# Hybrid decoder layer: transposes of the values and of some probabilities by GpSimd pieces and VectorE in place of TensorE

## The chip, the cores and the metric

One core of one Trainium2 chip runs the whole layer. The metric is the device time of one execution in microseconds, the median of several runs. One of the executions is recorded by the hardware profiler, and all durations of single instructions come from that one.

## The reference

One decoder layer on x of 2048 tokens by 1024 columns, all in float32. Cut to what matters:

```
h = rmsnorm(x, norm_pre_g);  z = h @ w_in                      # 1024 -> 4096 columns
q, k, v, g_attn, c_h, c_b, c_c, g_conv = split(z)              # 4 x 768 and 4 x 256 columns
q, k = rope(q), rope(k)                                        # 12 heads of 64
for window, dilation in ((128, 1), (512, 4), (2048, 16)):
    o_i, lse_i = dilated_window_attn(q, k, v, window, dilation)  # causal, keys at distance 0, d, .., window
o = sum(softmax(lse)_i * o_i)
attn_out = o * silu(g_attn)
conv_out = c_b * causal_conv3(c_c * c_h, conv_w) * silu(g_conv)
out = x + rmsnorm(concat(attn_out, conv_out) @ w_out, norm_post_g)
```

## The kernel before, in words

The tokens are cut into four chunks of 512 (b = 0 to 3 in the code, chunks 1 to 4 in the text), the columns of w_in into eight groups of 512. A unit is one group on one chunk, 32 in all, numbered n = 4 * group + chunk. Groups 0 and 7 are convolution units. Groups 1 to 6 are attention units: each has k, q, v and the gate of one pair of heads, so 24 units, p = 0 to 5 pairs on four chunks.

**Number format.** Operands of the large products are split into two parts, high and low, by a copy on ScalarE that rounds and a subtraction on VectorE that keeps the rest. A product is then three matmuls: high by high, high by low, low by high (L1072, L1073, L1074 for the input projection, L1241 to L1243 for the output projection, which uses seven products in place of eight on 2x2 blocks).

**An attention unit** (`attn_unit`, L669). The projection leaves k, q, v and gate in four PSUM banks. k and q are rotated on VectorE and GpSimd (L707, L711), split (L717, L718, L722, L723), and q is copied in another order of tokens by GpSimd (L727). v is copied to `vz` (L696, L698), transposed by four TensorE transposes of 128x128 into a PSUM bank (L739), and split from there by ScalarE and VectorE (L744, L745) into `v2`, which also goes to DRAM and comes back in another order as `v1` (L749, L752). Scores are made on TensorE with 64 rows per head (L772, L800), masked with a running minimum on VectorE (L779, L807) and exponentiated on ScalarE (L783, L811).

The three patterns are handled as two kinds of probabilities. Kind 1 is pattern 1, the window of 128: tiles `p1`, four blocks of 128 queries by 256 keys. Kind 4 are patterns 2 and 3 jointly, where keys that belong to both count twice: tiles `p4`, four residues by up to 512 keys. Both have queries on partitions, and the product with the values wants keys there, so they are transposed:

- `parts` (L818) does kind 4. Blocks of the two nearest chunks go through four TensorE transposes into a PSUM bank (L840) and are split from PSUM (L845, L846). Blocks further back (`far`, chunks 3 and 4 only) go without TensorE: their entries lie so that a transpose within 32x32 blocks by VectorE, in place in SBUF (L831), is enough, and they are split from SBUF (L832, L833).
- `square` (L851) does kind 1. The previous block is subtracted from the current one (L853), which is possible because the masks leave complementary triangles; one transpose per pair of blocks then serves both (L863), and ScalarE's Relu with scale 1 and -1 (L870) with a maximum and a minimum on VectorE (L873, L877) takes them apart from PSUM again.

The products with the values are L889 to L902, their results are gathered by L920, L923 and L925, weighted (L1017, L1018), joined and gated on GpSimd (L1019, L1020) and stored.

**What sets the order.** A planner (`Plan`, L131) takes every operation with an engine, an estimated duration, a priority and the tiles that it reads and writes, and simulates the five queues (TensorE, ScalarE, VectorE, GpSimd and SyncE's DMAs). The order that comes out is written out as a fixed order per engine. A table SHIFT (L119) moves priorities by place in the code and by unit; operations marked `port` are kept apart from each other in the plan. Projections of the next units fill TensorE between the steps of an attention unit. Eight PSUM banks (`st`) serve everything; the values' and probabilities' parts sit in rings of five (`v2`), three (`v1`) and three (`pt`), the convolution's work tile `u` exists once.

**The start.** The first weight tile is one DMA on SyncE's queue (L462), cast as a whole by ScalarE (L469) and subtracted by VectorE (L470); the first matmuls (L1061) need it and the first tile of x (L490). The remaining parts of x follow on SyncE's queue (L518).

Of the kernel before, what the change touches and what calls it, by code (L numbers as in the profile page):

```python
# [37 lines left out]
VISIT = 2  # L38
KT = D // 128
# [73 lines left out]
class Op:  # L113
# [230 lines left out]
def dmat(kb):  # L344
    return max(0.5, kb / 352.0)
# [3 lines left out]
def hybrid_layer(ctx: ExitStack, tc: tile.TileContext, x, w_in, w_out, conv_w, g_pre, g_post,  # L349
                 rope, consts, out):  # L350
    nc = tc.nc
# [96 lines left out]
    W, w_last = {}, []  # L448

    def weights_in(grp, i):  # L450
# [5 lines left out]
        if grp in (0, 7):  # L456
            W[grp, i] = w
            if grp or i:
                add("DMA", dmat(256), pr, lambda: nc.sync.dma_start(raw.ap, w_in[i, :, grp, :]), w=[raw], land=6.0 if grp else 3.6)
            else:  # L460

                add("DMA", dmat(256), -1.995e6, lambda: nc.sync.dma_start(raw.ap, w_in[i, :, grp, :]), w=[raw], land=3.6)  # L462
# [204 lines left out]
    first_attn = []  # L667

    def attn_unit(n, p, b, zs):  # L669
# [64 lines left out]
        ps, v2, v1 = Tok(st_r), Tok(v2_r), Tok(v1_r)  # L734
        V2[u], V1[u] = v2, v1

        def vt():
            for r in range(4):
                nc.tensor.transpose(ps.ap[:, r * 128:(r + 1) * 128], vz.ap[:, r * 128:(r + 1) * 128], ident)  # L739
        add("PE", 0.44, pr, vt, r=[vz, "cst"], w=[ps, (v2, "hold")], mode=2)  # L740

        def src():
            return ps.ap.rearrange("p (r h d) -> p r h d", r=4, h=2)
        add("ACT", actt(C, True), pr + URG, lambda: act.copy(v2.ap[:, :, 0:4:3, :], src()), r=[ps], w=[(v2, 0)])  # L744
        add("DVE", dvet(C), pr + URG, lambda: vec.tensor_tensor(  # L745
            v2.ap[:, :, 1:3, :], src(), f(v2.ap[:, :, 0:4:3, :]), op=ALU.subtract), r=[ps, (v2, 0)], w=[(v2, 1)])
# [70 lines left out]

        def parts(h, kind, blk, far=False):  # L818
            pt, m, pp = Tok(pt_r), len(blk), P[h, kind]
            tiles = sorted({a for a, _ in blk})  # L820
            if far:
# [7 lines left out]
                def cut(a):  # L829
                    return a.rearrange("p a (c q) -> p a c q", q=128)  # L830
                add("DVE", dvet(m * 128) + 0.05, pr, lambda: vec.transpose(src(), src()), w=[(pp, a) for a in tiles])  # L831
                add("ACT", actt(m * 128), pr + URG, lambda: act.copy(dst(0), cut(src())), r=[(pp, a) for a in tiles], w=[(pt, 0)])  # L832
                add("DVE", dvet(m * 128), pr + URG, lambda: vec.tensor_tensor(dst(1), cut(src()), f(dst(0)), op=ALU.subtract),  # L833
                    r=[(pp, a) for a in tiles] + [(pt, 0)], w=[(pt, 1)], port=True)
# [16 lines left out]
        def square(h):  # L851
            pp, ps, first = P[h, 1], Tok(st_r), int(b == 0)
# [8 lines left out]
            def tr():  # L861
                for g in range(4):
                    nc.tensor.transpose(ps.ap[:, g * 128:(g + 1) * 128], pp.ap[:, g, 128:], ident)  # L863
            add("PE", 0.436, pr, tr, r=[(pp, g) for g in range(4)] + ["cst"], w=[ps] + [(pt, "hold") for pt in two], mode=2)

            def p4(lo):
                return ps.ap[:, lo * 128:].rearrange("p (i c) -> p i c", c=128)
# [487 lines left out]
```

## Time and profile before

| What | us |
|---|---|
| median of 3 runs (lowest, highest) | 1165.99 (1165.15, 1166.27) |
| the profiled execution | 1165.18 |
| its span, first to last instruction | 1163.1 |
| TensorE busy | 1152.5 |
| VectorE busy | 960.3 |
| ScalarE busy | 668.2 |
| GpSimd busy | 199.7 |

The profile calls TensorE's matmuls PE and its weight loads PEld, VectorE DVE, ScalarE ACT, GpSimd POOL and SyncE SP. Busy time is the union of the recorded intervals of an engine. Matmuls are pipelined, so that their intervals overlap and a busy PE is not at its peak; what an instruction costs in a stream is better read from the distance of starts. A row of the groups gives line, engine, operation, tiles and shapes, count, then busy time and mean duration in ns, then idle time of the engine just before and what ended it. A row of the timeline gives start and duration.

The stretch from about 130 to 950 us holds the attention units, the time before it the first convolution group and the loading of x, the time after it the output projection. The granted TensorE clock of the profiled execution is 0.998.

### The profile page before, as it was taken

The page shows a single profiled execution, that of the slowest core. Times are in us where ns is not written, and L with a number is a line of the kernel's source. Part 1 is how long each engine was busy: PE and PEld are TensorE (multiplying, and loading weights), DVE is VectorE, ACT ScalarE, POOL GpSimd, SP SyncE. Part 2 cuts the span into 40 slices and gives each one's busy share as a digit, 9 for nine tenths or more (in the row PEclk, how much of TensorE's full clock was granted, in tenths as well). Part 3 has the DMA queues.
Part 4 walks back from the last instruction along what each step waited for, and adds up shares of the span by engine and source line. Part 5 has one row for each costly group of instructions (what it writes and reads, how often), then busy time and mean ns, then how long its engine had stood idle before and what let it go on. Part 6 is the DMA issues. An engine that isn't in the chain of part 4 may idle for free.

```text
span 1163.1 us, 19964 instructions
## 1 busy us (share of the span) xinstructions
PE 1152.5 (99%) x6422; PEld 958.3 (82%) x6422; DVE 960.3 (83%) x2424; ACT 668.2 (57%) x1722; POOL 199.7 (17%) x158
## 2 busy tenths in 40 slices
PE   9999999999999999999999999999999999999997
PEld 7888888888888888888888888888888888888885
DVE  4744588997999989898999998997999888688876
ACT  6743365665666556666665565674667454544442
POOL 0001112212131222121223221203222103000000
PEclk9999999999999999999999999999999999999999
DMA  9977786787688767777777767688776968445452
GB/s 345 391 278 261 247 247 212 226 236 230 203 247 269 234 215 227 238 223 242 232 245 229 252 167 247 204 272 260 228 243 199 318 208 297 156 149 178 152 165 91
DMA packets 174136, 269.39 MB, mean 232 GB/s; under 512 B 53584, under 2 KB 109904, under 8 KB 174032
## 3 DMA queue, kind: packets, MB, share of 16 engines
q1 hardware_dynamic: 173472, 267.85, 71.1%
q8 instruction: 51, 0.84, 0.3%
q14 instruction: 53, 0.43, 0.1%
q10 hardware_dynamic: 560, 0.27, 0.1%
HBM read 206.77 MB, written 48.69 MB: 220 GB/s over the span
## 4 chain that ended last, share of the span: by engine, by line
PE 94%; DVE 2%; ACT 2%; DMA 1%; SPq 0%; issue 0%; POOL 0%; DVEq 0%; POOLq 0%; ACTq 0%
PE st L1072 20%; PE st L1074 19%; PE st L1073 19%; PE st L889 5%; PE st L1241 4%; PE st L1243 4%; PE st L1242 4%; PE st L772 4%; PE st L800 3%; PE st L840 3%; PE st L901 2%; PE st L863 2%; PE st L548 1%; PE st L902 1%; PE st L739 1%; PE st L900 1%
## 5 line engine op out<-in xcount | busy, mean ns | idle before, releaser
L1072 PE MATMUL st<-xt,w 128*128 128x512 f32 x1020 | 413.3, 405 | 0.0
L1074 PE MATMUL st<-xt,w 128*128 128x512 f32 x1020 | 399.7, 392 | 0.0
L1073 PE MATMUL st<-xt,w 128*128 128x512 f32 x1020 | 398.3, 391 | 0.0
L1074 PEld LDWEIGHTS st<-xt,w 128*128 128x128 f32 x1020 | 191.5, 188 | 42.4
L1072 PEld LDWEIGHTS st<-xt,w 128*128 128x128 f32 x1020 | 191.9, 188 | 40.4 <-issue 6.7
L1073 PEld LDWEIGHTS st<-xt,w 128*128 128x128 f32 x1020 | 192.1, 188 | 31.1
L783 ACT ACTIVATE p<-p,sm 128x128 f32<-128x128 f32 (+3 forms) x192 | 105.9, 553 | 69.2 <-DVE sm L779 69.0
L925 DVE TENSOR_TENSOR uu<-st,uu 64x256 f32<-64x256 f32 x288 | 115.0, 418 | 26.0 <-ACT uu L920 21.8
L920 ACT COPY uu<-st 64x256 f32<-64x256 f32 x192 | 67.2, 367 | 100.7 <-PE st L889 55.9
L1019 POOL TENSOR_TENSOR uu<-uu 128x512 f32<-128x512 f32 x24 | 37.4, 1557 | 359.0 <-DVE uu L1018 359.0
L811 ACT ACTIVATE p<-p,e 128x256 f32<-128x256 f32 (+1 forms) x192 | 94.4, 495 | 5.0 <-DVE e L807 4.8
L779 DVE CUSTOM_DVE_ANT_0 p<-st,cst 128x128 f32<-128x128 f32 (+3 forms) x192 | 82.1, 485 | 16.1 <-PE st L772 15.7
L889 PEld LDWEIGHTS st<-pt,v 128*128 128x128 f32 x480 | 66.7, 191 | 5.6
L807 DVE CUSTOM_DVE_ANT_0 p<-st,cst 128x256 f32<-128x256 f32 (+1 forms) x192 | 66.8, 412 | 4.2 <-PE st L800 4.2
L889 PE MATMUL st<-pt,v 128*128 128x256 f32 x480 | 68.5, 283 | 0.0
L870 ACT ACTIVATE pt<-st 128x512 fp32r<-128x512 f32 (+1 forms) x96 | 51.1, 585 | 24.2 <-PE st L863 20.7
L707 DVE TENSOR_TENSOR rp<-rp,cs 128x512 f32<-128x512 f32 x72 | 53.7, 772 | 12.9 <-DMA rp<-rp 12.7
L707 POOL TENSOR_TENSOR rp<-rp,cs 128x512 f32<-128x512 f32 x24 | 39.5, 1646 | 143.1 <-DMA rp<-rp 96.9
L846 DVE TENSOR_TENSOR pt<-st,pt 128x512 fp32r<-128x512 f32 x84 | 55.9, 683 | 5.0 <-ACT pt L845 4.7
L772 PE MATMUL st<-kk,q 64*128 64x128 f32 (+3 forms) x576 | 56.3, 333 | 0.3 <-DVE v L745 0.2
L772 PEld LDWEIGHTS st<-kk,q 64*128 64x128 f32 x576 | 42.4, 185 | 15.1 <-issue 10.8
L845 ACT CAST pt<-st 128x512 fp32r<-128x512 f32 x84 | 46.8, 581 | 9.0 <-PE st L840 8.4
(262 smaller groups left out, 2045.6 us busy)
## 6 DMA issues: line engine op xcount, KB each, us to landing
xt<-xt SPq DMA_DIRECT2D x256, 512.0 KB
raw<-in_w_in SPq DMA_DIRECT2D x59, 256.0 KB
rp<-rp SPq DMA_DIRECT2D x192, 64.0 KB
vd<-v SPq DMA_DIRECT2D x24, 512.0 KB
v<-vd SPq DMA_DIRECT2D x96, 128.0 KB
ab<-ad SPq DMA_DIRECT2D x48, 256.0 KB
cs<-in_rope SPq DMA_DIRECT2D x19, 512.0 KB
uu<-mix SPq DMA_DIRECT2D x26, 256.0 KB
```

Source lines behind the costliest of these rows:

```text
L707: add(e, dur, pr, lambda o=o, a=a, i=i, eng=eng: eng.tensor_tensor(o.ap, a.ap, cs.ap[:, i], op=ALU.mult), r=[cs], w=[o], port=True)
L772: mm(ps[h].ap[:, (r - r0) * w:(r - r0 + 1) * w], Q.ap[lo:lo + 64, i, r * 128:(r + 1) * 128], KK[j][lo:lo + 64, 4 * r:4 * r + 4, 0:w // 4]. ...
L779: add("DVE", dvet(w) + 0.01, pr + URG, lambda h=h, r=r, P4=P4: vec.tensor_tensor_reduce(P4.ap[:, r, 0:w], ps[h].ap[:, (r - r0) * w:(r - r0 ...
L783: add("ACT", actt(w) + 0.19, pr, lambda h=h, r=r, P4=P4: act.activation(P4.ap[:, r, 0:w], P4.ap[:, r, 0:w], AF.Exp, bias=s4(0, h)[:, r:r + ...
L807: add("DVE", dvet(256) + 0.01, pr + URG, lambda h=h, j=j, g=g, P1=P1: vec.tensor_tensor_reduce(P1.ap[:, g, lo[g]:], ps[h].ap[:, j * 256 + ...
L811: add("ACT", actt(256 - lo[g]) + 0.19, pr, lambda h=h, g=g, P1=P1: act.activation(P1.ap[:, g, lo[g]:], P1.ap[:, g, lo[g]:], AF.Exp, bias=E ...
L889: mm(dst, v, pt.ap[:, i], start=c == 0, stop=c == b, skip_group_check=False)
L920: add("ACT", actt(256, True) + 0.09, pr + URG, lambda: act.copy(cols(a, lo), o()[hi:hi + 64, 0]), r=[O], w=[(a, (h, half))])
L925: fn = lambda l=l: vec.tensor_tensor(cols(a, lo), o()[lo:lo + 64, l], cols(a, lo), op=ALU.add)
L1072: mm(z.ap, w.ap[:, 0, js], xt.ap[:, 0], start=kt == 0, stop=False)
L1073: mm(z.ap, w.ap[:, 0, js], xt.ap[:, 1], start=False, stop=False)
L1074: mm(z.ap, w.ap[:, 1, js], xt.ap[:, 0], start=False, stop=kt == KT - 1)
```

## The change

Sixty groups of four TensorE transposes are replaced: the values of all 24 units, kind 1 of chunks 2 and 3 (24 squares), kind 4 of chunk 1 (12 tiles). In each, a tile of 128 partitions by four blocks of 128 columns is transposed in two steps. GpSimd copies sixteen pieces, each 32 partitions by four runs of 32 elements, so that the 32x32 blocks stand in each other's places; then VectorE transposes within the 32x32 blocks, in place. The parts are split from SBUF instead of PSUM. For the values the intermediate tile is the convolution's `u`; for the probabilities it is a part of the same `p1` or `p4` tile that is free by then. Kind 1 of chunks 1 and 4 and the near blocks of kind 4 in chunks 2 to 4 stay on TensorE.

Besides, the first weight tile is loaded in two halves, by SyncE's and ScalarE's queues, and its rounded parts are made by ScalarE and VectorE, half each; the load of g_pre moves behind the first x load on ScalarE's queue; a projection may be planned only behind all scores of the unit two before it; and the table SHIFT is a new one (65 entries, 58 before).

```diff
+MOVE = 0.37
+SWAP = "POOL"
+ONE, FOUR = (1,2,), (0,)
...
+                for h, (en, queue) in enumerate((("DMA", nc.sync), ("ACT", nc.scalar))):
+                    cl = slice(256 * h, 256 * h + 256)
+                    add(en, 0.45, -1.995e6, lambda cl=cl, queue=queue: queue.dma_start(raw.ap[:, cl], w_in[0, :, 0, cl]), w=[(raw, h)], land=3.2,
+                        data=0.0 if h else 0.4)
+                    eng, fn = (("ACT", act.copy), ("DVE", vec.tensor_copy))[h]
...
-        ps, v2, v1 = Tok(st_r), Tok(v2_r), Tok(v1_r)
+        v2, v1 = Tok(v2_r), Tok(v1_r)
...
-        def vt():
-            for r in range(4):
-                nc.tensor.transpose(ps.ap[:, r * 128:(r + 1) * 128], vz.ap[:, r * 128:(r + 1) * 128], ident)
-        add("PE", 0.44, pr, vt, r=[vz, "cst"], w=[ps, (v2, "hold")], mode=2)
+        vq = Tok(u_r)
+
+        def flat():
+            return vq.ap[:, 0:4].rearrange("p r c -> p (r c)")
+
+        def cells(t):
+            return t.rearrange("p (r c a) -> p r c a", r=4, c=4)
+        for c in range(4):
+            for a in range(4):
+                add("POOL", MOVE, pr, lambda a=a, c=c: pool.tensor_copy(
+                    cells(flat())[32 * a:32 * a + 32, :, c, :], cells(vz.ap)[32 * c:32 * c + 32, :, a, :]), r=[vz], w=[(vq, (a, c))])
+        add("DVE", dvet(C) + 0.05, pr, lambda: vec.transpose(flat(), flat()), w=[vq])
...
+        def swap(pp, src, dst):
+
+            def quarters(o):
+                return pp.ap[:, :, o:o + 128].rearrange("p g (c a) -> p g c a", c=4)
+            for c in range(4):
+                for a in range(4):
+                    add(SWAP, MOVE, pr, lambda a=a, c=c: (act.copy if SWAP == "ACT" else pool.tensor_copy)(
+                        quarters(dst)[32 * c:32 * c + 32, :, a], quarters(src)[32 * a:32 * a + 32, :, c]), r=[(pp, g) for g in range(4)], w=[(pp, ("q", a, c))])
+            add("DVE", dvet(C) + 0.05, pr, lambda: vec.transpose(pp.ap[:, :, dst:dst + 128], pp.ap[:, :, dst:dst + 128]),
+                w=[(pp, ("q", a, c)) for a in range(4) for c in range(4)] + [(pp, "t")])
...
+            elif b in FOUR:
...
+                for k in range(4):
+                    for a in range(4):
+                        add(SWAP, MOVE, pr, lambda a=a, k=k: (act.copy if SWAP == "ACT" else pool.tensor_copy)(
+                            split(place())[32 * k:32 * k + 32, :, :, a], split(given())[32 * a:32 * a + 32, :, :, k]),
+                            r=[(pp, x) for x in tiles], w=[(pp, ("q", half, a, k))], after=away)
+                add("DVE", dvet(C) + 0.05, pr, lambda: vec.transpose(place(), place()),
...
+            if b in ONE:
+                swap(pp, 128, 0)
+                ps = (pp, "t")
...
-    add("ACT", 0.45, -2.1e6, lambda: nc.scalar.dma_start(gp, g_pre), w=["gp"], land=4.0)
+    add("ACT", 0.45, -1.996e6, lambda: nc.scalar.dma_start(gp, g_pre), w=["gp"], land=3.6)
...
-              done = add("PE", 3 * mmt(C), n * 100 + 50 + (kt if conv else j // 2 * 4 + kt / 2), proj, r=[xt, w], w=[zs[j]])
+              done = add("PE", 3 * mmt(C), n * 100 + 50 + (kt if conv else j // 2 * 4 + kt / 2), proj, r=[xt, w], w=[zs[j]], after=scored.get(n - 2, ()))
```

More of the change, by code (lines that the diff above doesn't have):

```diff
@@ L445, in hybrid_layer @@
     URG = -1.0e5
-    W, w_last = {}, []
+    W, w_last, XW = {}, [], []
     def weights_in(grp, i):
@@ L460, in weights_in @@
             else:
-                add("DMA", dmat(256), -1.995e6, lambda: nc.sync.dma_start(raw.ap, w_in[i, :, grp, :]), w=[raw], land=3.6)
+                for h, (en, queue) in enumerate((("DMA", nc.sync), ("ACT", nc.scalar))):
[3 more added lines that the diff above has]
+                    eng, fn = (("ACT", act.copy), ("DVE", vec.tensor_copy))[h]
+                    XW.append(add(eng, actt(256) if h == 0 else dvet(256), URG - 151.9, lambda cl=cl, fn=fn: fn(w.ap[:, 0, cl], raw.ap[:, cl]), r=[(raw, h)], w=[(w, h)]))
+                w_last[:] = [add("DVE", dvet(C) + 0.01, pc, lambda: vec.tensor_tensor(w.ap[:, 1], raw.ap, f(w.ap[:, 0]), op=ALU.subtract),
+                                 r=[raw, (w, 0), (w, 1)], w=[(w, 2)], after=XH, port=True)]
+                return
         else:
@@ L731, in attn_unit @@
         products = ((0, 0), (0, 1), (1, 0))
-        ps, v2, v1 = Tok(st_r), Tok(v2_r), Tok(v1_r)
+        v2, v1 = Tok(v2_r), Tok(v1_r)
         V2[u], V1[u] = v2, v1
-        def vt():
-            for r in range(4):
-                nc.tensor.transpose(ps.ap[:, r * 128:(r + 1) * 128], vz.ap[:, r * 128:(r + 1) * 128], ident)
-        add("PE", 0.44, pr, vt, r=[vz, "cst"], w=[ps, (v2, "hold")], mode=2)
+        vq = Tok(u_r)
[8 more added lines that the diff above has]
+        add("DVE", dvet(C) + 0.05, pr, lambda: vec.transpose(flat(), flat()), w=[vq])
         def src():
[L743 to L746, printed above, removed]
+            return vq.ap[:, 0:4].rearrange("p r (h d) -> p r h d", h=2)
+        add("ACT", actt(C), pr, lambda: act.copy(v2.ap[:, :, 0:4:3, :], src()), r=[vq], w=[(v2, 0)])
+        add("DVE", dvet(C), pr, lambda: vec.tensor_tensor(
+            v2.ap[:, :, 1:3, :], src(), f(v2.ap[:, :, 0:4:3, :]), op=ALU.subtract), r=[vq, (v2, 0)], w=[(v2, 1)], port=True)
         d, dk = v_d[u % 2], ("vd", u % 2)
@@ L851, in square @@
         def square(h):
-            pp, ps, first = P[h, 1], Tok(st_r), int(b == 0)
+            pp, first = P[h, 1], int(b == 0)
             add("DVE", dvet(C), pr, lambda: vec.tensor_tensor(
@@ L859, in blocks, with p4, tr @@
                 return pts[:, sorted((pt_r.index(t.slot) for t in two), reverse=True)[s]]
[L861 to L867, printed above, removed]
+            if b in ONE:
+                swap(pp, 128, 0)
+                ps = (pp, "t")
+                def p4(lo):
+                    return pp.ap[:, lo:, 0:128]
+            else:
+                ps = Tok(st_r)
+                def tr():
+                    for g in range(4):
+                        nc.tensor.transpose(ps.ap[:, g * 128:(g + 1) * 128], pp.ap[:, g, 128:], ident)
+                add("PE", 0.436, pr, tr, r=[(pp, g) for g in range(4)] + ["cst"], w=[ps] + [(pt, "hold") for pt in two], mode=2)
+                def p4(lo):
+                    return ps.ap[:, lo * 128:].rearrange("p (i c) -> p i c", c=128)
+            on = b in ONE
             for s, pt in enumerate(two):
                 lo = first if not s else 0
-                add("ACT", actt((4 - lo) * 128, True), pr + URG, lambda lo=lo, s=s: act.activation(
-                    blocks(s)[:, lo:, 0, :], p4(lo), AF.Relu, scale=1.0 if s else -1.0), r=[ps], w=[(pt, 0)])
+                add("ACT", actt((4 - lo) * 128, not on), pr + URG, lambda lo=lo, s=s: act.activation(
+                    blocks(s)[:, lo:, 0, :], p4(lo), AF.Relu, scale=1.0 if s else -1.0), r=[ps], w=[(pt, 0)] + [(pt, "hold") for pt in two if on])
                 if s:
```

37 lines of the change are left out of this document (30 added, 7 removed), and 17 rows, old and new, of the table SHIFT.

## The prediction

> **What bounds the kernel now.** I read the page first: the busy shares and the chain that ended last.
>
> ```profile
> span 1163.1 us, 19964 instructions
> PE 1152.5 (99%) x6422; PEld 958.3 (82%) x6422; DVE 960.3 (83%) x2424; ACT 668.2 (57%) x1722; POOL 199.7 (17%) x158
> ...
> PE 94%; DVE 2%; ACT 2%; DMA 1%; SPq 0%; issue 0%; POOL 0%; DVEq 0%; POOLq 0%; ACTq 0%
> ```
>
> TensorE (PE) is busy 99% of the span and carries 94% of the chain. A busy PE need not be a PE at its peak, and a share of the whole span hides stages, so next came the windows: the stretch in which the attention units run (130 to 950 us), two short stretches inside it, and three successive units of one head pair. Columns: length, then PE, PEld, DVE, ACT and POOL busy us, then clock, DMA share, GB/s.
>
> ```profile
> 130.00:950.00 820.00, 819.35 (x4909) 684.34 (x4908) 727.01 (x1927) 504.34 (x1411) 178.58 (x143) 1.00 0.75 236
> 338.00:398.00 60.00, 60.00 (x353) 50.11 (x350) 58.09 (x138) 39.74 (x103) 13.64 (x10) 1.00 0.78 241
> 340.00:370.00 30.00, 30.00 (x168) 25.17 (x167) 29.48 (x66) 19.35 (x49) 7.25 (x6) 1.00 0.77 242
> 668.60:766.80 98.20, 98.20 (x600) 82.43 (x599) 86.34 (x235) 60.69 (x176) 21.67 (x18) 1.00 0.71 217
> ```
>
> In those 820 us PE lacks 0.65 us of being always busy: projection matmuls fill every hole, so work taken off PE there shortens the run, as long as nothing else becomes late. VectorE (DVE) is the next: 727.0 of 820 (88.7%), and for a while 58.09 of 60 (96.8%) or 29.48 of 30 (98.3%), with PE still full. GpSimd (POOL) has room: 178.6 of 820.
>
> **The change part by part: PE.** 24 units lose the four transposes of the values (L739). Of the squares (L863), chunks 2 and 3 of six head pairs with two heads, 24, lose four each. Of the joint probabilities (L840), chunk 1 with six pairs and two heads, 12, lose four each. That is 60 groups, 240 transposes. What a group costs is read from starts, since the recorded durations overlap. The timeline of PE, once without and once with a group between two L1074:
>
> ```profile
> 342.49 0.39 PE L1074 MATMUL st<-xt,w 128*128 128x512 f32 x1
> ...
> 343.17 0.39 PE L1074 MATMUL st<-xt,w 128*128 128x512 f32 x1
> ```
>
> ```profile
> 328.58 0.40 PE L1074 MATMUL st<-xt,w 128*128 128x512 f32 x1
> 328.81 0.60 PE L739 MATMUL st<-cst,rp 128*128 128x128 f32 x4
> ...
> 329.71 0.40 PE L1074 MATMUL st<-xt,w 128*128 128x512 f32 x1
> ```
>
> Three matmuls on from one L1074 is the next: 0.68 us without, 1.13 us with four transposes between. A group costs 0.45 us, 0.11 a transpose, and 60 groups 27.0 us. The busy time of these lines gives a little more (0.149 a transpose), because it counts tails under which the next matmul already runs:
>
> ```profile
> L863 PE MATMUL st<-cst,p 128*128 128x128 f32 x192 | 28.7, 272 | 0.0
> ```
>
> The Trainium skill, "TensorE: Matmul & The Clock Gate", Part 4, gives about 275 ns for one transpose inside a kernel; the 272 ns in this row agree. By that figure the estimate would be 66 us for 240. The starts decide here: 272 ns is the time through the array, and only 0.11 us of it holds up the next instruction.
>
> **VectorE.** Each group brings one transpose of 128x512 within 32x32 blocks, as chunks 3 and 4 have it at L831. The subtractions that follow read SBUF in place of PSUM:
>
> ```profile
> L831 DVE STREAM_TRANSPOSE p<-p 128x512 f32<-128x512 f32 x36 | 24.3, 696 | 0.6 <-ACT p L783 0.5
> ...
> L846 DVE TENSOR_TENSOR pt<-st,pt 128x512 fp32r<-128x512 f32 x84 | 55.9, 683 | 5.0 <-ACT pt L845 4.7
> ...
> L833 DVE TENSOR_TENSOR pt<-p,pt 128x512 fp32r<-128x512 f32 x36 | 26.4, 735 | 0.2
> ...
> L845 ACT CAST pt<-st 128x512 fp32r<-128x512 f32 x84 | 46.8, 581 | 9.0 <-PE st L840 8.4
> ...
> L832 ACT CAST pt<-p 128x512 fp32r<-128x512 f32 x36 | 22.1, 614 | 2.6 <-PE st L889 2.3 <-DVE p L831 0.2
> ```
>
> 24.3/36 = 0.675 us of busy time each, times 60: 40.5 us. L833 (from SBUF) means 735 against 683 at L846 (from PSUM); the 52 ns are not the source but a wait for POOL, next paragraph. ScalarE's copies get 33 ns dearer (614 against 581); 84 of them make 2.8 us on an engine that is busy 504 of 820 us, so nothing on the path, and at most 2.8 if that cover went.
>
> **The port between VectorE and GpSimd.** A DVE operation with two SBUF inputs and a POOL instruction exclude each other, single-input copies included:
>
> ```profile
> 361.16 0.61 POOL L727 CAST q<-q 128x512 fp32r<-128x512 f32 x1 [1.21 <-ACT q L722]
> ...
> 361.31 1.01 DVE L723 TENSOR_TENSOR q<-rp,q 128x512 fp32r<-128x512 f32 x1
> ```
>
> ```profile
> 421.40 1.67 POOL L1019 TENSOR_TENSOR uu<-uu 128x512 f32<-128x512 f32 x1 [21.01 <-DVE uu L1018]
> ...
> 421.84 1.78 DVE L707 TENSOR_TENSOR rp<-rp,cs 128x512 f32<-128x512 f32 x1
> ...
> 423.03 1.74 POOL L707 TENSOR_TENSOR rp<-rp,cs 128x512 f32<-128x512 f32 x1
> ```
>
> The copy ends at 361.77 and the DVE operation 0.55 us later; its undisturbed time is that of L846, 0.68, so the first 0.13 of a wait is hidden. In the second pair DVE ends at 423.62, again 0.55 after POOL's end, and the next POOL instruction waits: DVE gets the port at every hand-over, so a DVE operation waits for the rest of one copy, not for a row of sixteen.
>
> The change adds 960 copies (60 groups of 16, each 32 partitions by 128 elements). The trace has no such copy. From below stands a POOL instruction that writes one element per partition (102 ns), from above the copy of 512 elements over all partitions (median 617):
>
> ```profile
> L1346 POOL MEMSET const-bfloat16-1.0<- 128x1 bf16 x1 | 0.1, 102 | 0.0
> ```
>
> ```profile
> L727 POOL CAST q<-q x48: 611/617/1532, 133.0 to 898.4; 128x512 fp32r<-128x512 f32 x48
> ```
>
> A straight line between them gives 0.23 us at 128 elements. The planner books 0.37 (MOVE) and books 0.647 for L727, where the row has 0.617, so its POOL costs are good to 5%; I take 0.37 and keep 0.23 and 0.617 as ends. From the code, about 410 DVE operations with two SBUF inputs would run in the stage: eight per unit (192), 48 each at L470 and L853, 36 at L833, some 16 smaller groups' and the 84 subtractions that lose PSUM. With copies of length c the port is taken 960c of 792 us, and the mean excess of an operation that meets one is (c - 0.13) squared over 2c. At 0.37: 0.45 x 0.078 x 410 = 14 us. At 0.23: 2 us; at 0.617: 59 us.
>
> So DVE comes to 727.0 + 40.5 + 14 = 781.5 us, while PE needs 819.4 - 27.0 = 792.4: DVE would have to be busy 98.6% of the shorter stage. The trace shows it busy 96.8% for 60 us and 98.3% for 30 us with PE full, never that for the whole stage. I take the middle, 97.5%: 781.5/0.975 = 801.5 us, 18.5 less than now. PE then waits about 9 us that it did not wait before, for scores' banks and transposed probabilities that DVE delivers late.
>
> **GpSimd's own time and what queues behind it.** The row of three units above is chunks 1 to 3 of one pair. They get 48 copies each, 144 x 0.37 = 53 us on 21.7, so 75 of about 94 us. A copy that meets one of DVE's two-input operations (410 x 0.55 of 792 us, 28%) waits some 0.27 us, which makes it 0.445 on average: 86 of 94 us. Full, but not over. Behind the copies in POOL's order stand the rotation of q (L707, L711, L727) and the final combination (L1019, L1020); PE's scores wait for the first, nothing near waits for the second. The values now reach SBUF after 16 copies, a transpose and the split, some 6 us later than after 0.45 us of PE; SyncE waits for them at L749 already, and behind it stand the loads of the x tiles:
>
> ```profile
> SPq L749 <- DVE v L745: 25.4, 11, 5.5
> ```
>
> If the planner's order allows for 0.37 a copy, that is no cost; each copy 0.075 late makes 1.2 us per unit.
>
> **The rest.** Splitting the first weight load over two queues and engines lets the copy L469 end some 0.3 us earlier and so L490, for which the first matmul waits. But the chain then goes through the x load:
>
> ```profile
> 5.32 0.62 ACT L469 CAST w<-raw 128x512 fp32r<-128x512 f32 x1 [2.15 <-DMA raw<-in_w_in]
> ...
> 5.85 0.47 ACT L490 ACTIVATE xt<-st,gp 128x256 fp32r<-128x256 f32 x1
> ```
>
> ```profile
> 6.13 4.68 DMA p<-in_x
> ```
>
> PE stands until that lands (10.81), so I put 0, between -0.5 and +0.5 (the later g_pre). The 60 PSUM banks set free gain nothing while PE lacks 0.65 us. The edge from scores to the projection two units on lies within PE and holds no semaphore: 0. The new table of shifts reorders everything; it can gain at most those 0.65 us, and what it loses is in the range.
>
> Sum: span 1163.1 - 18.5 = 1144.6. The profiled execution took 1165.18, 2.1 around its span, and the median is 0.8 above it: 1166.0 - 18.5 = 1147.5 us.
>
> **The rivals.** (a) PE alone decides, DVE keeps up at 98.6%: 1166.0 - 27.0 = 1139. For it: the 30 us at 98.3%. Against it: no longer stretch holds that. (b) DVE takes all back: if it can hold no more than 781.5/820 = 95.3% over the stage, the time stays at 1166. Against it: the 60 us at 96.8%. (c) GpSimd becomes the bound, and slower: in chunks 1 to 3 it needs 144c + 21.7 us where the stage now has 98.2. From c = 0.53, waits included, it loses. At 0.55 it is 100.9, 2.7 over, times six pairs 16: 1182 us. For it: 0.445 is estimated and the 512-element copy takes 0.617; against it: a quarter of the elements. (d) The port is held for the whole of a copy and none of the wait is hidden: 0.45 x 0.185 x 410 = 34 us, DVE 801.5; at 97.5% the stage is 822, at 96.8% 828, so 1168 to 1174. Against it: L723 above ended 0.55, not 0.68, after the copy. The Trainium skill, "SBUF — State Buffer", "SBUF: two separate sides", has it so: an exclusive lock for the whole instruction, the loser fully blocked; the exclusion agrees with the rows, the full block does not quite. (e) SyncE's queue stands 1.2 us per unit longer at L749 and the x tiles come late by as much: 24 x 1.2 = 29, so 1147.5 + 29 = 1176.5. Against it: x tiles are fetched well ahead. That the transposes stay on PE can't be: the code drops them.
>
> **How the numbers follow.** DVE decides, 1141 to 1156 (781.5/0.983 = 795 and 781.5/0.968 = 807 us give 1141 and 1153, and the contention's upper end a little more): 0.47. (a) 0.24, (b) 0.08, (c) 0.11, (d) 0.05, (e) 0.05. Time 1147.5, range 1137 to 1178: outside lie (c) and the low edge of (a), about 0.15. About 0.2% is what a measurement here can tell from no change. Faster by more: 0.47 + 0.24 = 0.71; within: 0.08; slower: 0.11 + 0.05 + 0.05 = 0.21.
>
> **What would show it.** Right: L739 gone, L863 at 96 and L840 at 288; PE's lack in the attention stage grown from 0.65 us to about 9, ended by DVE (or by ACT behind it); DVE at 97 to 98% there; POOL's copies about 0.37 us with gaps, POOL busy near 600 us. Wrong: PE still without holes (a); POOL without gaps in chunks 1 to 3 and PE's holes ended by POOL (c); two-input DVE operations at a mean above 0.75 us (d); holes before L1072 ended by loads (e).

## The result, and the profile after

The changed kernel takes 1220.11 us (median of 4 runs, 1219.02 to 1221.62) against 1166.01 us before (4 runs, 1165.15 to 1166.27): 1.0466 times the time, interval 1.0448 to 1.0484. The forecast was 1147.5, the range ended at 1178. TensorE lost the work that it was to lose, and the run became 54 us longer.

The page of the kernel after: the span, the busy shares, and the chain that ended last, by engine and by line.

```profile
span 1217.4 us, 20561 instructions
PE 1165.3 (96%) x6182; PEld 945.4 (78%) x6182; DVE 1009.7 (83%) x2485; ACT 674.8 (55%) x1722; POOL 577.1 (47%) x1118
...
PE 44%; POOL 25%; DVE 21%; issue 4%; ACT 3%; DMA 3%; SPq 0%; DVEq 0%; POOLq 0%; ACTq 0%
POOL p L843 12%; PE st L1148 8%; PE st L1150 8%; PE st L1149 8%; POOL u L757 5%; PE st L1317 4%; PE st L1319 4%; PE st L1318 4%; POOL p L884 3%; DVE p L826 3%; DVE p L798 3%; DVE uu L999 2%; DVE rp L718 1%; POOL uu L1095 1%; PE st L559 1%
```

PE carried 94% of the chain before; now it carries 44%, and a quarter goes through GpSimd (POOL), an engine that is busy 47% of the span. Its three lines of copies are in the chain: L843 (pattern 1), L757 (values), L884 (joint probabilities). The window of the attention stage, in the same columns as before (PE, PEld, DVE, ACT, POOL busy us, then clock, DMA share, GB/s):

```profile
130.00:950.00 820.00, 779.50 (x4393) 628.93 (x4392) 720.84 (x1865) 482.35 (x1339) 529.15 (x1056) 0.98 0.71 217
338.00:398.00 60.00, 54.34 (x295) 42.13 (x294) 52.12 (x123) 33.18 (x85) 45.72 (x88) 1.00 0.70 225
```

PE now lacks 40.5 of 820 us, where it lacked 0.65. VectorE (DVE) isn't what fills up: 720.8 of 820, no more than before (727.0), in spite of its 60 transposes. GpSimd is busy 529 and idle 291 of 820 us. No engine is at its limit, so the next view has to be the waits. First the groups of the added operations and of the transposes left on PE:

```profile
L843 POOL COPY p<-p 32x128 f32<-32x128 f32 x384 | 165.1, 430 | 54.6 <-DVE p L917 38.6
L757 POOL COPY u<-rp 32x128 f32<-32x128 f32 x384 | 154.0, 401 | 18.9 <-DVE v L764 1.4
...
L884 POOL COPY p<-p 32x128 f32<-32x128 f32 x192 | 72.7, 379 | 24.6 <-ACT p L802 16.7
```

```profile
L904 PE MATMUL st<-cst,p 128*128 128x128 f32 x288 | 41.4, 278 | 0.9 <-DVE uu L997 0.9
...
L764 DVE TENSOR_TENSOR v<-u,v 128x512 fp32r<-128x512 f32 x24 | 18.6, 775 | 1.5 <-ACT v L763 1.4
...
L759 DVE STREAM_TRANSPOSE u<-u 128x512 f32<-128x512 f32 x24 | 17.0, 709 | 24.5 <-POOL u L757 24.2
L845 DVE STREAM_TRANSPOSE p<-p 128x512 f32<-128x512 f32 x24 | 17.0, 708 | 23.8 <-POOL p L843 23.8
...
L936 PE MATMUL st<-cst,p 128*128 128x128 f32 x96 | 14.8, 278 | 0.0
```

A copy takes (165.1 + 154.0 + 72.7)/960 = 0.408 us on average. The distribution behind it (from all 960 records) has two humps and a tail: three quarters take 0.28 to 0.31 us, with 0.33 us from one start to the next, most of the rest 0.6 to 0.8, beside a DVE operation with two SBUF inputs, and 18 take 1.0 to 3.5 us, 14 of these beside two to six such operations. The longest copy, and VectorE's operations beside it:

```profile
734.31 3.48 POOL L757 COPY u<-rp 32x128 f32<-32x128 f32 x1
```

```profile
734.22 0.67 DVE L897 TENSOR_TENSOR pt<-p,pt 128x512 fp32r<-128x512 f32 x1
734.81 0.68 DVE L1093 TENSOR_TENSOR uu<-uu,ab 128x512 f32<-128x512 f32 x1
735.41 0.68 DVE L1094 TENSOR_TENSOR uu<-uu,ab 128x512 f32<-128x512 f32 x1
736.01 1.02 DVE L917 TENSOR_TENSOR p<-p 128x384 f32<-128x384 f32 x2
736.95 0.68 DVE L734 TENSOR_TENSOR q<-rp,q 128x512 fp32r<-128x512 f32 x1
```

VectorE's six operations follow one another without a pause, and the copy ends only behind the last of them. So a row of 16 takes from its first start to its last end 8.4 us for pattern 1, 10.1 for the values (other GpSimd work stands between) and 7.4 for the joint probabilities, where the planner books 16 x 0.37 = 5.9.

The last column of L759 and L845 is the new thing: VectorE stands 24.2 and 23.8 us behind the copies. The view of waits has the same from the side of the waiters (total us, times, longest):

```profile
ACT v L763 <- DVE u L759: 42.0, 17, 6.0
...
ACT pt L944 <- DVE p L845: 35.9, 14, 4.4
...
ACT q L733 <- POOL rp L722: 29.8, 11, 5.5
DVE u L759 <- POOL u L757: 24.2, 13, 5.4
DVE p L845 <- POOL p L843: 23.8, 16, 3.4
DVE p L887 <- POOL p L884: 5.3, 4, 2.9
```

Two things wait for GpSimd: the transposes (53.3 us together, and ScalarE behind them), and the rotation of q, which goes through GpSimd at L722. In the kernel before, the longer waits for GpSimd were these two (the others make 1.2 us):

```profile
ACT q L722 <- POOL rp L711: 13.5, 9, 4.0
...
DVE g L661 <- POOL u L660: 5.4, 4, 1.5
```

One place shows how this gets to PE. First GpSimd alone, then all engines:

```profile
230.01 2.52 POOL L843 COPY p<-p 32x128 f32<-32x128 f32 x6
232.62 1.28 POOL L1095 TENSOR_TENSOR uu<-uu 128x512 f32<-128x512 f32 x1
233.96 1.33 POOL L843 COPY p<-p 32x128 f32<-32x128 f32 x2
235.38 1.62 POOL L1096 TENSOR_TENSOR uu<-uu,g 128x512 f32<-128x512 f32 x1
237.06 5.97 POOL L843 COPY p<-p 32x128 f32<-32x128 f32 x17
```

```profile
239.71 0.71 DVE L845 STREAM_TRANSPOSE p<-p 128x512 f32<-128x512 f32 x1 [3.41 <-POOL p L843]
...
240.45 0.77 DVE L999 TENSOR_TENSOR uu<-st,uu 64x256 f32<-64x256 f32 x2
240.51 0.63 ACT L944 ACTIVATE pt<-p 128x512 fp32r<-128x512 f32 x1 [4.43 <-DVE p L845]
...
241.02 0.97 PE L791 MATMUL st<-kk,q 64*128 64x512 f32 x6 [3.34 <-DVE uu L999]
```

The row of copies is cut by two combinations of 1.3 and 1.6 us. VectorE stands 3.41 us at the transpose. Behind the transpose in its order is L999, which empties banks of earlier products; it waits for nothing itself. PE's scores need one of those banks, so PE stands 3.34 us. The next rows are the windows just behind that hole, and a later one:

```profile
242.10:245.50 3.40, 3.29 (x10) 2.26 (x11) 3.34 (x10) 2.10 (x6) 3.07 (x9) 0.50 0.44 112
246.00:249.40 3.40, 3.40 (x18) 2.84 (x18) 3.40 (x13) 3.38 (x11) 2.94 (x11) 1.00 0.16 31
```

From 242.1 us the granted clock is 0.50 for 3.4 us: 10 matmuls where the later window has 18. Seven such stretches (six of 3.4 us, one of 10.2) add up to 30.7 us, half of which, 15, is lost. Before, the clock is at half only at the very end. So the hole of 3.34 us costs 1.7 more behind it. A shorter one can be enough: at 397.88 PE had stood 1.71 us, 2.1 from start to start, and the clock was at half from 399.1; two of the seven stretches follow two or three holes of 0.7 to 1.6 us in a row. A hole of 2.0 us from start to start at 457.5 is followed by none.

```profile
395.79 0.39 PE L1150 MATMUL st<-xt,w 128*128 128x512 f32 x1
397.88 0.36 PE L974 MATMUL st<-pt,v 128*128 128x256 f32 x1 [1.71 <-ACT pt L864]
```

The Trainium skill, "TensorE: Matmul & The Clock Gate", "HAM oscillation — how this bites in real kernels", warns of gaps of the array above some 3.4 us; the stretches of 3.4 us agree with that window, but here about half of it sufficed.

How a hole falls matters too. The seven stretches start whole multiples of 3.413 us after one another (46, 31, 11, 40, 31 and 24 of them). If the span is cut into such steps, PE was busy for 0.7 to 2.1 us in the step in front of each stretch. Three other steps had as little (1.81, 1.90 and 2.06 us) and were followed by full clock.

What came off and what came on can be read from the distances between PE's starts, each compared with the median distance behind a matmul of the same shapes and tiles in the kernel before. The transposes that are gone make 26 us of such usual distances. Outside the half-clock stretches, 53 starts come more than 0.35 us late and hold 54 us (4 with 3 us before), and those 0.1 to 0.35 us late hold 40 us (27 before). The half-clock stretches hold 16 us of lateness. So 1163.1 - 26 + 51 + 13 + 16 = 1217, and the span is 1217.4: about the forecast 27 us came off, and 80 us of holes, small delays and half clock came on.

### The profile page after: what moved, and what is told of

It reads as the page before. It is cut to its first block, busy times and chain, and to the rows that moved or that the text cites. A ratio compares the mean times of both kernels' runs of the same rounds, so it can differ in the third digit from the quotient of the medians.

```text
span 1217.4 us, 20561 instructions
## 1 busy us (share of the span) xinstructions
PE 1165.3 (96%) x6182; PEld 945.4 (78%) x6182; DVE 1009.7 (83%) x2485; ACT 674.8 (55%) x1722; POOL 577.1 (47%) x1118
## 4 chain that ended last, share of the span: by engine, by line
PE 44%; POOL 25%; DVE 21%; issue 4%; ACT 3%; DMA 3%; SPq 0%; DVEq 0%; POOLq 0%; ACTq 0%
POOL p L843 12%; PE st L1148 8%; PE st L1150 8%; PE st L1149 8%; POOL u L757 5%; PE st L1317 4%; PE st L1319 4%; PE st L1318 4%; POOL p L884 3%; DVE p L826 3%; DVE p L798 3%; DVE uu L999 2%; DVE rp L718 1%; POOL uu L1095 1%; PE st L559 1%
## 5 line engine op out<-in xcount | busy, mean ns | idle before, releaser
L843 POOL COPY p<-p 32x128 f32<-32x128 f32 x384 | 165.1, 430 | 54.6 <-DVE p L917 38.6
L757 POOL COPY u<-rp 32x128 f32<-32x128 f32 x384 | 154.0, 401 | 18.9 <-DVE v L764 1.4
L999 DVE TENSOR_TENSOR uu<-st,uu 64x256 f32<-64x256 f32 x288 | 113.7, 417 | 12.2 <-ACT uu L994 8.4
L884 POOL COPY p<-p 32x128 f32<-32x128 f32 x192 | 72.7, 379 | 24.6 <-ACT p L802 16.7
L718 POOL TENSOR_TENSOR rp<-rp,cs 128x512 f32<-128x512 f32 x24 | 32.5, 1352 | 100.6 <-DMA rp<-rp 71.0
L671 POOL TENSOR_TENSOR u<-rp,rp 128x512 f32<-128x512 f32 x8 | 17.1, 2132 | 132.1 <-DVE rp L666 91.1
L791 PE MATMUL st<-kk,q 64*128 64x128 f32 (+3 forms) x576 | 64.0, 346 | 13.4 <-DVE uu L999 4.0
L722 POOL TENSOR_TENSOR rp<-rp,rp 128x512 f32<-128x512 f32 x24 | 33.2, 1385 | 63.6 <-DVE rp L718 62.6
```

The source lines that it names most:

```text
L757: add("POOL", MOVE, pr, lambda a=a, c=c: pool.tensor_copy(cells(flat())[32 * a:32 * a + 32, :, c, :], cells(vz.ap)[32 * c:32 * c + 32, :, ...
L791: mm(ps[h].ap[:, (r - r0) * w:(r - r0 + 1) * w], Q.ap[lo:lo + 64, i, r * 128:(r + 1) * 128], KK[j][lo:lo + 64, 4 * r:4 * r + 4, 0:w // 4]. ...
L843: add(SWAP, MOVE, pr, lambda a=a, c=c: (act.copy if SWAP == "ACT" else pool.tensor_copy)(quarters(dst)[32 * c:32 * c + 32, :, a], quarters ...
L884: add(SWAP, MOVE, pr, lambda a=a, k=k: (act.copy if SWAP == "ACT" else pool.tensor_copy)(split(place())[32 * k:32 * k + 32, :, :, a], spli ...
L999: fn = lambda l=l: vec.tensor_tensor(cols(a, lo), o()[lo:lo + 64, l], cols(a, lo), op=ALU.add)
```

## The experiments

Each run is one execution beside one of the kernel before on the same chip; the latter took 1165.1 to 1169.3, so the column of differences is what to compare. Executions of the kernel after differ by up to 2.6 us, so a difference under about 3 us can't be told from none. The runs e1 to e5, e9, e10, e12 and e16 keep the order of the kernel after. The memset runs leave out the moves, that is, the data does not get to its place. "Piece" is the mean time of one copy, or of what stands for it.

| run | piece us | time | before | difference |
|---|---|---|---|---|
| e5 memsets, no transposes | 0.197 | 1149.79 | 1166.39 | -16.6 |
| e1 memsets of 128 elements | 0.197 | 1160.12 | 1166.12 | -6.0 |
| e2 copies of 4 elements | 0.290 | 1164.29 | 1166.12 | -1.8 |
| e10 memsets of 4 x 64 | 0.305 | 1167.38 | 1169.34 | -2.0 |
| the change | 0.408 | 1220.11 | 1166.01 | +54.1 |
| e9 memsets of 4 x 102 | 0.433 | 1237.29 | 1169.34 | +68.0 |
| e16 as e9, nobody waits for them | 0.438 | 1202.35 | 1167.39 | +35.0 |
| e12 as e9, nobody waits, ring held | 0.433 | 1252.48 | 1165.10 | +87.4 |
| e3 only the values' copies short | | 1195.87 | 1166.12 | +29.7 |
| e4 only the squares' copies short | | 1186.35 | 1166.12 | +20.2 |
| e6 planned with 0.45 a copy | 0.391 | 1219.28 | 1166.39 | +52.9 |
| e13 that plan, memsets of 4 x 64 | 0.304 | 1195.92 | 1165.10 | +30.8 |
| e14 4 of 16 pieces on ScalarE | 0.418 | 1201.25 | 1165.10 | +36.2 |
| e15 8 of 16 pieces on ScalarE | 0.430 | 1221.29 | 1165.10 | +56.2 |
| e11 before, joint probabilities alone | 0.328 | 1175.12 | 1169.34 | +5.8 |
| e7 before, 800 unread copies | 0.340 | 1186.41 | 1166.39 | +20.0 |
| e8 before, 50 unread transposes | | 1169.54 | 1166.39 | +3.1 |

**The pieces' time: e1, e2.** The copies become memsets of the same pieces, or shrink to four elements; order, waits and transposes stay.

```diff
-add("POOL", MOVE, pr, lambda a=a, c=c: pool.tensor_copy(
-    cells(flat())[32 * a:32 * a + 32, :, c, :], cells(vz.ap)[32 * c:32 * c + 32, :, a, :]), ...
+add("POOL", MOVE, pr, lambda a=a, c=c: pool.memset(
+    cells(flat())[32 * a:32 * a + 32, :, c, :], 0.0), ...
```

```diff
-    cells(flat())[32 * a:32 * a + 32, :, c, :], cells(vz.ap)[32 * c:32 * c + 32, :, a, :]), ...
+    cells(flat())[32 * a:32 * a + 32, :, c, 0:1], cells(vz.ap)[32 * c:32 * c + 32, :, a, 0:1]), ...
```

> Left out: the moves. Each of the 960 copies is a memset of the same piece, so GpSimd writes but reads nothing; every engine's order and every wait are those of the changed kernel. Theory A (lateness through the port: copies locked out by VectorE's two-input operations come late, VectorE stands in its order at the transpose behind them, TensorE gets holes and loses its clock): if a memset needs no read port, the pieces run without waits, VectorE's idle time behind GpSimd falls from 58 us to under 15, and the time to 1140 to 1155. Theory B (VectorE's added 40 us of transposes is the bound): nothing changes for VectorE, 1195 to 1220. Theory C (the new order itself is bad, whatever the pieces take): 1205 to 1220.

> Left out: most of the moves. Each copy moves 4 in place of 128 elements per partition; the order and the waits are those of the changed kernel. Theory A: the pieces still take the read port, but for about 0.1 us less, so 16 need about 3.7 us in place of 8 to 10; VectorE's idle time behind GpSimd falls to 10 to 25 us and the time to 1140 to 1165. Theory B: 1195 to 1220. Theory C: 1205 to 1220.

1160.12 and 1164.29: the loss is gone with the copies' time, and VectorE's load and the new order by themselves don't cost it. In the memset run no piece is longer than 0.2 us, and VectorE stands 6.2 us behind GpSimd in all (5.4 before, 57.6 in the kernel after).

**One kind at a time: e3, e4.** The same shrinking for the values alone (384 copies) and for the squares alone (384).

> Left out: most of the moves of the values alone (384 of the 960 copies are of 4 elements); the order is that of the changed kernel. Theory A: the loss goes with lateness and each group of copies has its share; the values are wanted late (they go through DRAM), so their own lateness is cheap, but they stand ahead of the probabilities' copies in GpSimd's queue: about a third of the gain of the run with all copies short, 1185 to 1205. Rival: the values alone hold everything up (their tile exists once): nearly the whole gain, 1145 to 1170. Theories B and C: 1205 to 1220.

> Left out: most of the moves of pattern 1's probabilities alone (384 of the 960 copies are of 4 elements); the order is that of the changed kernel. Theory A: these are wanted at once by the products with the values, and their transposes stand in VectorE's order in front of the emptying of the score banks: half or more of the gain of the run with all copies short, 1170 to 1195. Theories B and C: 1205 to 1220.

1195.87 and 1186.35: 24 and 34 us of the 54 go with one kind. Both matter, and the two savings together (58) are about that of all three kinds (56): no single place is to blame.

**What PE's part alone is worth: e5.** Memsets as in e1, and the 60 transposes are left out.

```diff
-add("DVE", dvet(C) + 0.05, pr, lambda: vec.transpose(flat(), flat()), w=[vq])
+add("DVE", dvet(C) + 0.05, pr, lambda: None, w=[vq])
```

> Left out: the moves (memsets of the same pieces, which read nothing) and VectorE's 60 transposes behind them; every order and all other waits are those of the changed kernel. With memsets alone the time was 1160, 21 above what TensorE would need (1139). Theory B2 (those 21 us are VectorE's added load of 40 us): it falls to 1138 to 1147. Theory C2 (they are the new order, whatever VectorE has to do): 1154 to 1161.

1149.79, between the two ranges. The transposes cost 10.6 us (from -16.6 to -6.0), and even without them and with cheap pieces 27.0 - 16.6 = 10.4 us of PE's gain don't arrive. PE's starts tell where they are, though not why: compared as above, those more than 0.35 us late hold 5 us more than before, the smaller delays 7. So 1139 was not to be had in this order.

**The booked price: e6.** MOVE = 0.45 and an empty table of shifts; the planner lays out the whole kernel anew.

> The full change, but the planner books 0.45 us for each copy, which is what it takes on the chip with its waits, in place of 0.37, and the table of shifts is empty, so the order is a new one. Theory A1 (the loss is the plan's wrong price; an order made with the true one has no holes): TensorE's idle time behind VectorE falls below 15 us and the time to 1145 to 1166. Theory A2 (there is no room: with the true price the plan itself is long, because VectorE and GpSimd exclude each other and each unit's chain has three more steps): 1180 to 1210.

1219.28: booked 0.45, the copies took 0.391, and the kernel is as slow. So theory A1's gain does not come. But the run changes two things, the price and the table of shifts, so alone it doesn't show that the price has no effect; e13 below separates the two.

**Load without anybody waiting: e7, e8.** To the kernel before, with its order, come 800 copies (or 50 transposes) on an idle tile, in the places where the groups' sources are ready; PE keeps its transposes.

```diff
+def extra(after, pr):
+    add("POOL", 0.0, pr, pieces, after=after)
...
+p < 5 and extra([o for o in pl.ops if vz in o.toks], pr)
```

> The kernel before with TensorE's transposes, plus 50 groups of 16 copies (800, of constants into a tile that is idle then) on GpSimd, about where the change has them in pairs 1 to 5; nobody waits for them but GpSimd's own later work. Theory A: VectorE loses little directly at the port (410 operations, some 7 to 14 us in all, on an engine with slack), GpSimd's q rotation and combination come some us later: 1166 to 1178. Rival (VectorE's own waits at the port are what costs): 1190 or more.

> The kernel before with TensorE's transposes, plus 50 transposes of 128x512 on VectorE in place in an idle tile, about where the change has them in pairs 1 to 5; nobody waits for them. It adds 34 us to VectorE and takes nothing from TensorE. Theory B2 (VectorE has no room for its added load without holes in TensorE): 1175 to 1195. Rival (VectorE's 11% of idle time takes them): 1166 to 1172.

The 34 us of transposes cost VectorE 23 us more busy time in the stage (749.98 of 820) and the run 3 us, hardly more than the noise. The unread copies cost 20 us, more than theory A's range and less than the rival's, though VectorE's two-input operations were stretched by 7 us only, summed as for the kernel after under "Why the prediction was wrong". Where it went, from the timeline of the copies' run:

```profile
129.94 1.61 POOL L723 TENSOR_TENSOR rp<-rp,rp 128x512 f32<-128x512 f32 x1
131.50 6.12 POOL L401 COPY u<-cst 32x128 f32<-32x128 f32 x16
137.69 1.17 POOL L739 CAST q<-q 128x512 fp32r<-128x512 f32 x2
```

```profile
138.35 1.03 PE L813 MATMUL st<-kk,q 64*128 64x128 f32 x6 [2.36 <-POOL q L739]
```

Sixteen copies stand 6.12 us in GpSimd's order between the rotation and the cast of q; PE's scores wait 2.36 us for the cast, and the clock drops to half at 138.5. GpSimd's own work behind the copies is a path to PE.

**Port or lateness: e9, e10.** The short memsets read nothing, and none of them waits (none takes over 0.21 us); copies do both, so e1 and e2 leave it open whether the copies' time or their contention with VectorE costs. A memset that lasts as long as a copy with its waits tells them apart.

```diff
+    flat()[32 * a:32 * a + 32].rearrange("p (r c) -> p r c", r=4)[:, :, 0:102], 0.0), ...
```

> The kernel after with its own order and waits, and each of the 960 copies replaced by a memset of 32 rows x 4 x 102 elements of the tile that the copy wrote (nothing is read, and the moves are left out). In the short memset run a piece was 32 rows x 128 elements, took 0.197 us and never waited; a GpSimd memset of one element took 0.10 us in it, so an estimate for 408 elements is 0.10 + 408 x 0.76 ns = 0.41 us, about the mean of the copies in the kernel after (0.38 to 0.43 us) with their waits. Theory A (pieces that are late by their mean time leave VectorE, which takes its work in order, standing at the transpose; whether the time goes into reading or into waiting does not matter): 1200 to 1225 us, VectorE idle behind GpSimd 40 us or more, TensorE holes over 0.6 us 40 or more. Rival P (it is the contention of copies and VectorE for the port): GpSimd's memsets wait for no VectorE operation, so VectorE's two-input operations are stretched as little as before and the run stays at 1158 to 1170 us.

> As the run with memsets of 102 elements a row, but 32 rows x 4 x 64 elements a piece: an estimate of 0.10 + 256 x 0.76 ns = 0.295 us, about an undisturbed copy (0.29 us), and below the 0.37 us that the plan books. Theory A (only pieces later than the plan has them cost): 1160 to 1168 us. Rival P: 1158 to 1165 us; so this run says where the rise begins, not which theory holds.

The groups of memsets, first 4 x 64, then 4 x 102 elements a row:

```profile
L843 POOL MEMSET p<- 32x256 f32 x384 | 117.3, 305 | 57.9 <-DVE p L917 36.8 <-ACT uu L994 1.3
```

```profile
L843 POOL MEMSET p<- 32x408 f32 x384 | 166.3, 433 | 62.5 <-DVE p L917 42.7
```

e9 takes 1237.29, above even theory A's range (1200 to 1225) and far above rival P's; e10 takes 1167.38, in theory A's. In e9 no piece reads and none waits (433 ns is the mean, 428 the least, 443 the most). VectorE's subtractions and additions with two SBUF inputs of 128x512 take 0.681 us on average where they overlap memsets alone (168 of them) and 0.682 where they overlap no GpSimd instruction; beside copies alone, in the kernel after, they take 0.718. So the contention between pieces and VectorE is gone, and the loss is greater. It is the pieces' time; the port matters mainly in that it makes a copy of 0.29 us one of 0.41. From 0.305 to 0.433 us a piece the run grows by 70 us, for 0.128 x 960 = 123 us of GpSimd time; from 0.197 to 0.305 it grows by 4, for 104 us. The waits for GpSimd at the two ends of that rise, 4 x 64 first:

```profile
ACT q L733 <- POOL rp L722: 8.8, 7, 1.9
DVE u L759 <- POOL u L757: 4.4, 4, 2.7
...
DVE p L845 <- POOL p L843: 0.9, 2, 0.6
```

```profile
ACT q L733 <- POOL rp L722: 34.2, 10, 6.1
DVE p L845 <- POOL p L843: 31.5, 15, 4.2
DVE u L759 <- POOL u L757: 31.3, 17, 6.2
```

**Who waits: e12, e16.** The long memsets again, but the transposes turn, and the splits read, other tiles, so nobody waits for a piece.

```diff
-vec.transpose(pp.ap[:, :, dst:dst + 128], pp.ap[:, :, dst:dst + 128])
+vec.transpose(pp.ap[:, :, src:src + 128], pp.ap[:, :, src:src + 128])
```

> The run with memsets of 102 elements a row (0.433 us a piece, 1237 us), with one difference: the 60 VectorE transposes turn, and the splits and Relu read, the tile that the copies read in the kernel after, so nobody waits for a piece (the moves are left out). GpSimd's queue has the same 960 pieces at the same places. Theory A1 (the time is lost where VectorE and ScalarE wait for the pieces at the transpose): 1160 to 1180 us. Rival A2 (it is lost because GpSimd's own operations, the rotation, the casts of q and the mixes, come late behind the pieces): 1205 to 1235 us.

> As the first run with unread long memsets, except that the values' split reads a constant tile (and a VectorE copy of 512 elements a row stands for the values' transpose), so that no slot of the rotation's ring is held longer than in the run where the pieces are read (1237 us); GpSimd's queue has the same 960 memsets of 0.433 us, and nobody waits for them (the moves are left out). Theory A1 (the time is lost where VectorE and ScalarE wait for the pieces): 1160 to 1185 us. Rival A2 (it is lost because GpSimd's own operations come late behind the pieces): 1205 to 1237 us. In between: the share of each.

e12 answers another question than the one put: its values read the rotation's ring for longer, its loads came late, and VectorE stood 53 us behind loads (9 to 10 us in e9 and in the kernel after). e16 reads a constant tile there and takes 1202.35. Against -6.0 with short memsets, the long ones cost 41 us when nobody waits for them and 74 when the transposes do. Two things differ besides: the copy that stands for the values' transposes takes 0.43 us (median) where a transpose takes 0.71, and 20 memsets beside that copy take 0.60 to 0.74 us. So neither theory holds alone: GpSimd's own operations behind the pieces account for somewhat over half, the waits at the transposes for the rest, as far as two such parts can be told apart when a hole of one can hide one of the other. The waits of e16:

```profile
ACT q L733 <- POOL rp L722: 55.9, 13, 5.9
PEld st L819 <- POOL q L738: 6.5, 4, 3.3
PE st L819 <- POOL q L738: 5.2, 2, 2.9
```

**The plan that books 0.45, with cheap pieces: e13.**

> The order planned with 0.45 us a copy and an empty table of shifts (with copies: 1219 us), each copy replaced by a memset of 0.305 us that reads nothing (the moves are left out). Theory A (what costs is the pieces' time, and only beyond what VectorE's order can wait for): 1175 to 1190 us, about what the plan itself says, 1185. Rival O (the order of that plan is bad whatever the pieces take): 1205 to 1220 us.

1195.92, between the ranges: 30.8 us are that order's own, at pieces a third cheaper than booked, and 22 are the copies' time above 0.304 us. In the order of the change the copies' time above 0.305 us costs 56 (from -2.0 to +54.1). So the higher price did take away more than half of that loss, in an order that, with the empty table of shifts, is worse elsewhere by about as much.

**Sooner groups: e14, e15.** Four, or eight, of each 16 pieces go to ScalarE.

```diff
-add("POOL", MOVE, pr, lambda a=a, c=c: pool.tensor_copy(
+add("ACT" if (c + a) % 4 < 1 else "POOL", actt(128) if (c + a) % 4 < 1 else MOVE, pr,
+    lambda a=a, c=c: (act.copy if (c + a) % 4 < 1 else pool.tensor_copy)(
```

> The whole change, nothing left out, but of each group of 16 pieces 4 are copied by ScalarE and 12 by GpSimd; planned anew with 0.45 us a GpSimd copy and an empty table. A group then takes GpSimd 12 x 0.42 = 5.0 us where it took 16 x 0.42 = 6.7 us, and GpSimd has 100 us less. Theory A: most of the loss comes back, 1165 to 1195 us. Rival (a fixed cost of each group, the hand-over from GpSimd to VectorE, or VectorE's load decides): 1205 us or more.

> As the run before it with 8 pieces on ScalarE and 8 on GpSimd: 3.4 us a group on GpSimd. ScalarE has 480 copies more, 120 to 150 us (its copies of like size are not in the traces so far; 0.25 to 0.3 us each is an estimate from the 0.366 us of its 64 x 256 copies). Theory A: 1160 to 1190 us, no more than the split by four; if ScalarE becomes the late one, 1190 to 1215 us.

1201.25, 6 us above theory A's range, and 1221.29, 31 us above it and above the case where ScalarE is late. The first gives back a third of the loss of e6, the second nothing. ScalarE's copies take 0.296 us, so they aren't cheaper; at 8 of 16 it is busy 622 of 820 us (482 in the kernel after) and VectorE stands 143 us behind it (96 in the kernel after, 114 in e6). This fits a late ScalarE in place of a late GpSimd; no run shows it by itself.

**The smallest part: e11.** The kernel before with its table, and only the joint probabilities of chunk 1 moved (192 copies).

> The kernel before with one part of the change alone: the joint probabilities of chunk 1 (12 groups, 192 copies, 12 transposes), values and pattern 1 as before, and the table of shifts of before. Nothing is left out. TensorE has 12 x 0.45 = 5.4 us less. Theory A (copies arrive 0.05 to 0.1 us late each, on a stretch where GpSimd has gaps: a group 1 to 1.5 us late, a part of it before a VectorE that stands): 1166 to 1180 us, slower than before or the same. Rival C (a part this small keeps the gain of TensorE): 1158 to 1163 us.

1175.12, in theory A's range but not by its mechanism: the copies take 0.328 us, 0.366 from start to start, as booked, and PE has 817.7 of 820 us in the stage. The holes are behind it: PE stands 3.5 us at L1277, behind ScalarE, at about 1001 us, and the clock is at half for 6.8 us from 1003.6. Why that place comes late wasn't tried further. No version tried that moves the data itself beats the kernel before.

## Why the prediction was wrong

**The step that failed** is the one on GpSimd: "86 of 94 us. Full, but not over", and "If the planner's order allows for 0.37 a copy, that is no cost; each copy 0.075 late makes 1.2 us per unit". It counted throughput. The sum itself was fair: a copy forecast at 0.445 with its waits measured 0.408, and 0.42 to 0.48 from start to start; GpSimd was forecast near 600 us and has 577. But GpSimd and VectorE take their work in order. GpSimd is idle 291 of 820 us because the operation at the head of its queue waits for VectorE, ScalarE or a load (276, 77 and 82 us over the whole span), so the free third can't be used when a row of copies is late; the rotation of q and the combinations stand behind the row, and VectorE stands at the transpose with the emptying of PE's banks behind it. A row takes 7.4 to 10.1 us where 5.9 are booked, so it is late by 1.5 to 4 us, and nothing in the order covers that. The prediction had both queues in its text ("PE's scores wait for the first") and priced them at 1.2 us a unit, 29 us at most, as a delay of x tiles. The runs put 41 us on GpSimd's own queue and 33 on the transposes, for pieces of 0.433 us, and the half clock behind the holes is part of both.

**PE's 27.0 us** came off about as worked out: L739 is gone, L936 has 96, L904 has 288, and the account above gives 26. But e5 shows that this order, with cheap pieces and no transposes, gets 16.6 of it.

**VectorE** did not become the bound: forecast 97 to 98% busy, measured 87.9% (720.8 of 820). The transposes' price (0.675 us) was right: 0.709. What they cost the time is 10.6 us by e5 and e1, and 3.1 by e8 where nobody waits.

**The port** was sized about right for VectorE, and its other side was counted only as GpSimd's load. VectorE's two-input operations that overlap a GpSimd instruction stand 35 us before and 47 after beyond the median of those of their kind that overlap none: 12 us more, where 14 were forecast; 8 of them fall on the maxima and minima of L947 and L951, which now read SBUF. On the other side the port lengthens a GpSimd copy from 0.29 to 0.41 us on average. The prediction gave a copy that meets VectorE 0.27 us of waiting, though its own reading, that VectorE gets the port at every hand-over, lets a copy wait for a row of operations, as the 3.48 us above show. The longer mean brought the pieces from the flat part of the curve (0.305: -2.0 us) to the steep one (0.408: +54).

**The rivals.** (c) is the nearest, GpSimd as the bound and slower; it got 0.11. Its point of decision was put at 0.53 us a copy by throughput, and the runs turn between 0.305 and 0.408. Its sign, PE's holes ended by GpSimd, would have missed it: PE's idle time is ended by DVE (35.4 us) and by POOL for 1.2 only; GpSimd is two steps back in the chain. (a) and (b) are out. The sign of (d) is there, two-input operations at 775 ns at L764, but the 12 us more are about a third of its 34. (e) isn't seen: SyncE does stand longer for the values (52.4 us at L768, 25.4 before), but PE's idle time in the stage is ended by VectorE and ScalarE, not by loads.

**What stays open**: why the 10.4 us that e5 lacks don't arrive, how exactly the loss divides between GpSimd's own queue and the transposes, and how far a table of shifts found for the true durations would bring the change; no such table was searched for.

## What to carry to other kernels

An engine that is half idle can still set the end if it takes its work in order: before moving a step to it, list what stands behind the step in that queue and who waits for it, and ask how late the step may be, not how much time the engine has left. A step that leaves an engine that is always fed for one that shares a port gets a spread of durations, and in a kernel planned to the tenth of a microsecond the mean of that spread, not the undisturbed time, has to fit. To tell load from lateness, put an operation of the same length without the data in its place: two lengths of a memset showed here between which durations the loss sets in.

## What the runs showed of the hardware

A GpSimd copy of 32 partitions by 128 fp32 elements takes 0.29 us undisturbed, one of 4 elements 0.19, and 0.33 us pass from start to start of two copies in a row; beside one VectorE operation with two SBUF inputs it mostly takes 0.6 to 0.8, beside several in a row up to 3.48. Memsets of the same rows take 0.197, 0.305 and 0.433 us for 128, 256 and 408 elements and hardly spread (0.428 to 0.443 for the longest in e9): beside VectorE's two-input operations they don't wait, and these take as long as alone (0.681 and 0.682 us for 128x512). So GpSimd's write alone didn't contend with these here, a read and write did. Beside a VectorE copy from SBUF to SBUF (L759 in e16, one input) 20 such memsets did stretch, to 0.60 to 0.74 us. ScalarE's copy of the same piece takes 0.296 us. And PE's granted clock fell to 0.50 for 3.41 us, or two or three times that, behind steps of 3.41 us in which PE was busy for 2.4 us at most; in every run the starts of these stretches lie whole multiples of 3.413 us apart.
